# Rotation tables of a state-space scan: made per unit at their use, or all eight ahead of time and kept in DRAM

## The chip, the cores and the metric

The kernel runs on one core of a Trainium2 chip. The metric is the device time of one execution in microseconds (us), the median of several runs. The engines are named as in the profile: PE (TensorE, matmuls), DVE (VectorE), ACT (ScalarE), POOL (GpSimd) and SP (SyncE, which here issues most DMAs). Each engine, and each DMA queue, takes its instructions in the order in which they stand in its row.

## The reference

It is one layer of a hybrid decoder for 512 prompt tokens (plus 16 meta tokens) and 8 sample tokens. All of them share the weights. An attention branch and an S5 state-space branch run in parallel on parts of one projection, and are merged. What matters here is the state-space branch:

```python
lam_bar = jnp.exp(lam * dt)
b_bar = ((lam_bar - 1.0) / lam)[..., None] * lax.complex(b_re, b_im)
bu = jnp.einsum('gph,btgh->btgp', b_bar, uf)
a_cum, h = lax.associative_scan(ssm_combine, (a, bu), axis=1)
y = jnp.einsum('ghp,btgp->btgh', c, h).real + d_skip * uf
```

`lam_bar` is a complex number per group and state. The recurrence h(t) = lam_bar h(t-1) + bu(t) is linear.

## The kernel before, in words

**Stages.** The span has five stages. From 0 to 113 us the first blocks of the input projection run, each a product of a 2048 x 128 slice of weights with all tokens. From 113 to 416 us come 15 "quads" (`quad`, `Quads`): groups of four blocks of 1024 x 128 weights that are computed with seven products in place of eight, from sums of weight blocks and sums of token blocks. From 430 to 730 us come the remaining projection blocks with the state-space units between them, then attention up to 1096 us, and the output projection in quads again.

**A product** takes fp32 numbers as two parts of lower precision. For each 128 x 128 tile of weights PE does three matmuls, 24 in a product: `pr<-...,whi` twice and `pr<-...,wlo` once (L1382, in `product`). The weight parts are made just ahead (`Quads.make`, `Quads.load`): SP loads `raw` from DRAM; where a sum of weight blocks is needed DVE adds two of them (L1073, `raw<-raw`); ACT casts `raw` to `whi` (L1074); DVE subtracts, `wlo = raw - whi` (L1075), the "split". Six places for `raw` and five pairs of places for `whi` and `wlo` are used in turn. So DVE has to give one split per product, and PE's later products wait for it. DVE also adds up the results of a quad (L1417, L1422, L1432) and scales them (L1200); SP stores them to `gD`.

**Background work.** Everything else is written as Python generators (`Background`), of which `step` advances some at each product according to a credit: a `yield` names the cost of the piece before it, `yield None` ends the turn, and GBUDGET is the credit given per product. That sets the program order. A scheduler then makes each engine's row out of it, with weight work at a high priority, so that rows differ from the program order; semaphores keep what depends on each other in order. `later()` stands for `tc.issue_after(bg.last)`: what is issued inside it is to be issued after PE's latest product matmul.

**ssm_prep** runs in the background of the quads, on POOL (class `OnPool`), with small operations (mostly 128 x 32 and 128 x 64) in `work` tiles, two flat rooms `flats[0]` and `flats[1]` of 2144 numbers a partition. It computes `lam`, its powers, the factors `Fk`, and two tables of powers of the unit-modulus part of `lam_bar`: T6 (exponents 0 to 5) and T11 (multiples of 6, eleven of them). The function `powers` makes each; `norm` (L239 to L243) scales it to modulus one at the end, for T11 with operations 704 wide (L240, L243). T6[j] times T11[i] is the rotation for step 6i + j of a segment of L = 66 steps. The kept values (KEPT, 1920 numbers a partition) are stored to DRAM with one DMA of POOL's queue after the 14th quad, because x's parts need the room, and loaded again after the quads.

**ssm_consts** prepares one of eight units (four groups of states on 128 partitions each) in the state-space stage, on DVE and ACT, and at its end makes the unit's rotation table `tab` (L404 to L419): four outer products T11 x T6 (L412), a subtraction (L415) and a negated addition (L419), all 128 x 264 on DVE. **ssm_block** does the unit: PE computes bu; DVE rotates it with `tab` (p1, p2, L483 and L484; w, L488 and L489, for each half of the unit apart); scans with the real decay (L503), which leaves a scan without complex numbers; and rotates back, for each of NB = 2 segments apart (L509, L510: two products 528 wide; L512, L513: two sums 264 wide). PE then makes y.

Of the kernel before, what the change touches and what calls it, by code (L numbers as in the profile page):

```python
# [8 lines left out]
F32 = mybir.dt.float32  # L9
# [3 lines left out]
ALU = mybir.AluOpType  # L13
AX = mybir.AxisListType
P = 128
L = 66
NB = 2
NC = 132
# [49 lines left out]
def cmul(v, pool, out, a, br, bi, sh, tag):  # L68
# [13 lines left out]
KEPT = (("prm", (3, 32)), ("lam", (2, 32)), ("lamp", (2, 4, 32)), ("Fk", (8, 32)), ("nF", (2, 32)), ("r4", (32,)),  # L82
        ("T6", (2, 32, 6)), ("T11", (2, 32, 11)), ("car", (2, 32)))
NKEPT = sum(int(np.prod(s)) for _, s in KEPT)

# [51 lines left out]

def kept(ap):

    r, o = {}, 0  # L140
    for nm, sh in KEPT:
# [7 lines left out]
def ssm_prep(nc, K, tmp, psum, dram, R, ident, a_prm, later):  # L149

    v = OnPool(nc, tmp)
    prm = K["prm"]
# [4 lines left out]
    t = tmp.tile([P, 32], F32, name="th")  # L157
# [10 lines left out]
    yield 3.0  # L168
    x = tmp.tile([P, 32], F32, name="xr")
# [4 lines left out]
    v.tensor_tensor(out=th, in0=aim, in1=dt, op=ALU.mult)  # L174
    yield 3.0

# [31 lines left out]
    v.tensor_tensor(out=lam, in0=e1, in1=bc(rho, 1, 2), op=ALU.mult)  # L208
    yield 3.0

# [17 lines left out]
    v.tensor_scalar(out=nF, in0=fv[:, :, 0], scalar1=-1.0, scalar2=None, op0=ALU.mult)  # L228
    yield 2.5

# [14 lines left out]
    def powers(tab, z, cnt, tag):  # L245

        v.memset(tab[:, 0, :, 0], 1.0)
        v.memset(tab[:, 1, :, 0], 0.0)
        zs = [z]
        for i in range(3):  # L250
            nz = tmp.tile([P, 2, 32], F32, name=f"{tag}z{i}")
            cmul(v, tmp, nz, zs[-1], zs[-1][:, 0], zs[-1][:, 1], (32,), "c32_")
            zs.append(nz)
        n = 1
        for zp in zs:
            m = min(n, cnt - n)
# [5 lines left out]
            yield 1.5  # L262
        norm(tab, (32, cnt), "nt")
        yield 2.0
        return zs
# [16 lines left out]
    car = K["car"]  # L282
    v.tensor_tensor(out=car, in0=c2, in1=bc(r4, 1, 2), op=ALU.mult)
    yield 1.0
    for _ in range(8):
        yield None
# [11 lines left out]
    R["FD"] = FD  # L298
    yield 0.0


# [21 lines left out]
def ssm_consts(nc, pool, dram, R, D, ub, a_bT, a_bN, a_cT, e32, d_skip, later, free):  # L323
# [40 lines left out]
    B = pool.tile([P, 2, 512], F32, name="B")  # L364
    nc.sync.dma_start(out=B, in_=a_bT[ub])
    CL = pool.tile([P, 4, 2, 5, 32], F32, name="CL")
    nc.scalar.copy(out=CL[:, :, :, 0], in_=c)
# [35 lines left out]

    tab = pool.tile([P, 2, 4, L], F32, name="tab")  # L404
    x = R["T11"][:, :, ps]
    y = R["T6"][:, :, ps]
    t1 = pool.tile([P, 4, 11, 6], F32, name="rt1", bufs=1)
    t2 = pool.tile([P, 4, 11, 6], F32, name="rt2", bufs=1)
    tv = tab.rearrange("p r a (i j) -> p r a i j", j=6)

    def outer(dst, i, j):
        v.tensor_tensor(out=dst, in0=bc(x[:, i], 3, 6), in1=bc(y[:, j], 2, 11), op=ALU.mult)  # L412
    outer(t1, 0, 0)
    outer(t2, 1, 1)
    v.tensor_tensor(out=tv[:, 0].rearrange("p a i j -> p (a i j)"), in0=t1.rearrange("p a i j -> p (a i j)"),  # L415
                    in1=t2.rearrange("p a i j -> p (a i j)"), op=ALU.subtract)
    outer(t1, 0, 1)
    outer(t2, 1, 0)
    v.scalar_tensor_tensor(out=tv[:, 1].rearrange("p a i j -> p (a i j)"), in0=t1.rearrange("p a i j -> p (a i j)"),  # L419
                           scalar=-1.0, in1=t2.rearrange("p a i j -> p (a i j)"), op0=ALU.mult, op1=ALU.subtract)  # L420
    D["tab"] = tab
# [4 lines left out]
    D["d0"] = d0  # L426
    yield 2.4

# [15 lines left out]
def ssm_block(nc, pool, R, D, ub, y_out, later):  # L444
# [26 lines left out]
    yield 0.0  # L471
    yield None
    for h in range(2):
        p1 = pool.tile([P, 2, 2, NB, L], F32, name="p1", tag="rt1", bufs=1)
        p2 = pool.tile([P, 2, 2, NB, L], F32, name="p2", tag="rt2", bufs=1)
        for i in range(2):
            parts = [(slice(0, 2), bu[2 if h else i][:, 0:280].rearrange("p (e c) -> p e c", e=2))]
            if (h, i) == (1, 1):
                parts = [(slice(e, e + 1), place(1, 1, e).unsqueeze(1)) for e in range(2)]
            for es, b in parts:  # L480
                a = slice(2 * h + es.start, 2 * h + es.stop)
                bi = b[:, :, 0:NC].rearrange("p e (n l) -> p e n l", l=L)
                v.tensor_tensor(out=p1[:, i, es], in0=bi, in1=bc(tab[:, 0, a], 2, NB), op=ALU.mult)  # L483
                v.tensor_tensor(out=p2[:, i, es], in0=bi, in1=bc(tab[:, 1, a], 2, NB), op=ALU.mult)  # L484
                g = slice(4 * ub + a.start, 4 * ub + a.stop)
                v.tensor_tensor(out=R["sst"][:, g, i], in0=R["A0"][:, g, i], in1=b[:, :, NC:140], op=ALU.add)
        wv = w[:, :, 2 * h:2 * h + 2].rearrange("p n a r l -> p r a n l")
        v.tensor_tensor(out=wv[:, 0], in0=p1[:, 0], in1=p2[:, 1], op=ALU.subtract)  # L488
        v.tensor_tensor(out=wv[:, 1], in0=p1[:, 1], in1=p2[:, 0], op=ALU.add)  # L489
        yield 3.0  # L490
    tre, tim = bc(tab[:, 0], 2, 2), bc(tab[:, 1], 2, 2)
    for n in range(NB):
# [12 lines left out]
        yield 1.3 + 0.8 * n  # L505
    for n in range(NB):
        t1 = pool.tile([P, 4, 2, L], F32, name="rt1", bufs=1)
        t2 = pool.tile([P, 4, 2, L], F32, name="rt2", bufs=1)
        v.tensor_tensor(out=t1, in0=w[:, n], in1=tre, op=ALU.mult)  # L509
        v.tensor_tensor(out=t2, in0=w[:, n], in1=tim, op=ALU.mult)  # L510
        hs = slice(9 + n * L, 9 + n * L + L)
        v.tensor_tensor(out=H[:, :, 0, hs], in0=t1[:, :, 0], in1=t2[:, :, 1], op=ALU.add)  # L512
        v.tensor_tensor(out=H[:, :, 1, hs], in0=t2[:, :, 0], in1=t1[:, :, 1], op=ALU.subtract)  # L513
        yield 2.2
    for i, sg in ((0, 1.0), (1, -1.0)):
# [416 lines left out]
BUDGET = 6.4  # L932
GBUDGET = 0.4
BUDGET2, BUDGET3, BUDGET4 = 6.0, 3.4, 4.8
# [154 lines left out]
def trunk(tc, A, O):  # L1089
# [396 lines left out]
    def xpart(k, c):  # L1486
# [5 lines left out]
    flats = [xp.tile([P, 8 * CH], F32, name="work", tag=n) for n in ("xhq", "xlq")]  # L1492
    bg.add(ssm_prep(nc, kept(flats[0][:, 0:NKEPT]), Places([flats[1], flats[0][:, NKEPT:]], spots()), aux, dram, S, C["idn"],
                    A["prm"], lambda: tc.issue_after(bg.last)))
    kD = dram.tile([P, NKEPT], F32, name="kept")

# [453 lines left out]
```

## Time and profile before

| what | us |
|---|---|
| three runs | 1263.16, 1266.23, 1267.95 (median 1266.23) |
| span of the profiled execution (its whole time is not listed apart) | 1262.3 |
| PE busy | 1250.9 (99%) |
| DVE busy | 980.6 (78%) |
| ACT busy | 628.7 (50%) |
| POOL busy | 266.1 (21%) |
| all waits of PE for DVE in the quads | 0.2 |
| waits of PE in the state-space units | 0.6, 0.6, 0.5 |

A row of a form (a group of instructions of one line, operation and shape) reads: line, engine, operation, output <- inputs, shapes, how often; then busy time in us, mean in ns, idle time ahead of them on the engine, and what ended it. A row of the timeline reads: start, duration, what; in brackets the idle time before it and what released it. A row of a window reads: from, to, length, then busy time of PE, PE's weight loads, DVE, ACT and POOL with the number of instructions of each, PE's granted clock, the busy share of the DMA engines, and GB/s.

### The profile page before, as it was taken

How to read it: one execution, taken by the hardware profiler on the slowest of the kernel's cores; microseconds unless marked ns; L12 is line 12 of the kernel's file. 1: busy time of each engine (PE TensorE's matmuls, PEld its weight loads, DVE VectorE, ACT ScalarE, POOL GpSimd, SP SyncE). 2: the span in 40 equal slices, each digit the busy share in tenths (PEclk: the TensorE clock that was granted, in tenths of full speed). 3: DMA queues.
4: the chain of work that ended last, by engine and by line, in shares of the span. 5: the costliest groups of instructions: out<-in, count | busy, mean ns of one | idle time of the engine just before them, and what ended most of it. 6: DMA issues, size and time to landing. Idle time of an engine off the chain costs nothing.

```text
span 1262.3 us, 26537 instructions
## 1 busy us (share of the span) xinstructions
PE 1250.9 (99%) x10357; PEld 1227.7 (97%) x10357; DVE 980.6 (78%) x1554; ACT 628.7 (50%) x1344; POOL 266.1 (21%) x437
## 2 busy tenths in 40 slices
PE   9999999999999999999999999999999999999998
PEld 9999999999999999999999999999999999999998
DVE  8687878887778668888897377899887577887875
ACT  8554445444545586556432235567555333344342
POOL 0003999940000033122220123211011000000000
PEclk9999999999999999999999989999999999999999
DMA  8544343443434656555554775777666756555441
GB/s 294 199 160 153 134 143 110 143 150 134 151 126 146 214 172 182 159 165 167 156 159 121 246 211 182 224 240 225 189 214 203 258 174 189 165 192 163 145 139 51
DMA packets 108001, 219.22 MB, mean 174 GB/s; under 512 B 21932, under 2 KB 47492, under 8 KB 107844
## 3 DMA queue, kind: packets, MB, share of 16 engines
q1 hardware_dynamic: 99172, 198.53, 48.5%
q0 software_dynamic: 8704, 19.00, 5.6%
q8 instruction: 81, 1.33, 0.4%
q14 instruction: 44, 0.36, 0.1%
HBM read 181.57 MB, written 36.82 MB: 173 GB/s over the span
## 4 chain that ended last, share of the span: by engine, by line
PE 92%; DVE 3%; DMA 2%; ACT 1%; SPq 1%; issue 0%; DVEq 0%; ACTq 0%
PE mm L1168 45%; PE pr L1382 35%; PE wg L854 2%; PE mm L1255 2%; PE aux L1382 1%; PE aux L1168 1%; PE aux L1255 1%; DVE wlo L1009 1%; PE aux L806 1%; PE aux L805 1%; ACT ct L346 1%; PE tr L526 1%; PE tr L836 1%; PE wg L526 1%; DMA Y<-yD 0%
## 5 line engine op out<-in xcount | busy, mean ns | idle before, releaser
L1075 DVE TENSOR_TENSOR wlo<-raw,whi 128x1024 fp32r<-128x1024 f32 x161 | 198.5, 1253 | 69.6 <-ACT whi L1074 69.0
L1074 ACT CAST whi<-raw 128x1024 fp32r<-128x1024 f32 x161 | 166.4, 1049 | 167.2 <-DVE raw L1073 80.0
L1168 PE MATMUL mm<-xh,whi 128*128 128x260 f32 (+1 forms) x792 | 185.8, 288 | 3.1 <-DVE t L563 2.9
L1008 ACT CAST whi<-raw 128x1024 fp32r<-128x1024 f32 (+3 forms) x128 | 122.3, 965 | 132.3 <-PE mm L1168 85.6
L1168 PE MATMUL mm<-xh,wlo 128*128 128x260 f32 (+1 forms) x792 | 184.4, 287 | 0.0
L1168 PE MATMUL mm<-xl,whi 128*128 128x260 f32 (+1 forms) x792 | 184.1, 286 | 0.0
L1009 DVE TENSOR_TENSOR wlo<-raw,whi 128x1024 fp32r<-128x1024 f32 (+3 forms) x128 | 142.2, 1119 | 46.5 <-ACT whi L1008 45.7
L1382 PE MATMUL pr<-tau,whi 128*128 128x260 f32 x928 | 168.6, 283 | 0.0
L1382 PE MATMUL pr<-cb,whi 128*128 128x260 f32 x848 | 153.0, 283 | 0.0
L1382 PEld LDWEIGHTS pr<-tau,whi 128*128 128x128 f32 x928 | 143.0, 188 | 0.0
L1168 PEld LDWEIGHTS mm<-xh,whi 128*128 128x128 f32 x792 | 132.5, 189 | 5.8 <-ACT KH L747 3.1
L1168 PEld LDWEIGHTS mm<-xl,whi 128*128 128x128 f32 x792 | 133.1, 190 | 0.4 <-issue 0.4
L1168 PEld LDWEIGHTS mm<-xh,wlo 128*128 128x128 f32 x792 | 132.2, 189 | 0.4 <-issue 0.4
L1382 PEld LDWEIGHTS pr<-cb,whi 128*128 128x128 f32 x848 | 130.8, 188 | 0.2 <-ACT z L1416 0.2
L1382 PE MATMUL pr<-tau,wlo 128*128 128x260 f32 x464 | 130.8, 282 | 0.0
L1382 PE MATMUL pr<-cb,wlo 128*128 128x260 f32 x424 | 119.1, 283 | 0.2 <-DVE wlo L1075 0.2
L1073 DVE TENSOR_TENSOR raw<-raw 128x1024 f32<-128x1024 f32 x91 | 113.9, 1252 | 1.6
L1168 PE MATMUL mm<-Y,whi 128*128 128x260 f32 x576 | 105.1, 287 | 0.0
L1382 PE MATMUL pr<-xl,whi 128*128 128x260 f32 x352 | 98.9, 283 | 0.0
L1382 PE MATMUL pr<-xh,wlo 128*128 128x260 f32 x352 | 98.8, 283 | 0.0
L1382 PE MATMUL pr<-xh,whi 128*128 128x260 f32 x352 | 97.1, 283 | 0.0
L1382 PEld LDWEIGHTS pr<-tau,wlo 128*128 128x128 f32 x464 | 87.2, 188 | 0.0
(421 smaller groups left out, 2974.9 us busy)
## 6 DMA issues: line engine op xcount, KB each, us to landing
raw<-in_w SPq DMA_DIRECT2D x202, 512.0 KB, 4.3
gD<-z SPq DMA_DIRECT2D x34, 260.0 KB, 4.3
t<-gD SPq DMA_DIRECT2D x32, 260.0 KB, 3.1
cache<-in_vc POOLq DMA_DIRECT2D x16, 286.0 KB, 3.5
cache<-in_kc POOLq DMA_DIRECT2D x15, 288.0 KB, 4.0
xr<-in_x SPq DMA_DIRECT2D x16, 268.0 KB, 6.5
xg<-in_x SPq DMA_DIRECT2D x8, 536.0 KB, 4.7
sbw<-rawD SPq DMA_DIRECT2D x16, 260.0 KB, 5.1
```

The costliest lines, as they stand in the source:

```text
L346: nc.scalar.activation(out=dst, in_=src, func=AF.Copy, scale=x)
L526: nc.tensor.matmul(o[n], lhsT=D["CL"][:, 2 * e + n, i, 1:5], rhs=H[:, 2 * e + n, i, 0:140], start=False, stop=(i == 1))
L805: nc.tensor.matmul(ps[:, e, 0:272], lhsT=q, rhs=KH[:, k0:k0 + 272], start=True, stop=False)
L854: nc.tensor.matmul(pv[64 * e:64 * e + 64, 0:256], lhsT=V, rhs=pr[:, e::2], start=(i == 0), stop=(i == len(parts) - 1))
L1008: nc.scalar.copy(out=hi, in_=raw)
L1009: self.dve = nc.vector.tensor_tensor(out=lo, in0=raw, in1=hi.bitcast(F32), op=ALU.subtract).ins
L1073: nc.vector.tensor_tensor(out=o, in0=o, in1=i, op=ALU.add)
L1074: nc.scalar.copy(out=hi, in_=t)
L1075: nc.vector.tensor_tensor(out=lo, in0=t, in1=hi.bitcast(F32), op=ALU.subtract)
L1168: m = nc.tensor.matmul(ps[:, c, 0:W], lhsT=wt[:, k], rhs=xo(kt, c), start=f, stop=l)
L1255: nc.tensor.matmul(ps[:, c, 0:260], lhsT=wt[:, kt % 8], rhs=xk(xo, kt, c, 8), start=f, stop=l)
L1382: m = nc.tensor.matmul(bank, lhsT=wt[:, p], rhs=x(p, e), start=first and f and p == 0, stop=l and p == 7, skip_group_check=not first and l ...
```

## The change

T6 and T11 leave the kept values, so that the DMA that stores and loads them is 832 numbers a partition in place of 1920. At the end of `ssm_prep` all eight rotation tables are made, on DVE, in `room`, which is `flats[1]`: into `t[0]` the products with one of T6's two parts, into `t[1]` those with the other, combined in place in `t[0]`. Each table is stored twice side by side (r = 0, 1) into `tabD` in DRAM by two DMAs of SP's queue, in pieces of 66 numbers (264 bytes), 1024 pieces and 264 KB each. The yields of `ssm_prep` are about halved, the pause ahead of `ft` goes from 8 to 14 turns, and GBUDGET from 0.4 to 0.5. `ssm_consts` no longer makes the table, but loads it with one DMA. `ssm_block` takes both halves in one subtraction and one addition (528 wide), and both segments in one operation each of the rotation back (1056 and 528 wide).

```diff
-        ("T6", (2, 32, 6)), ("T11", (2, 32, 11)), ("car", (2, 32)))
+        ("car", (2, 32)))
+MADE = KEPT + (("T6", (2, 32, 6)), ("T11", (2, 32, 11)))
...
-    for _ in range(8):
+    for _ in range(14):
         yield None
...
+    R["tabD"] = dram.tile([8, P, 16 * L], F32, name="tabD")
+    t = [f.rearrange("p (r a i j) -> p r a i j", r=2, a=4, j=6) for f in (room[:, 0:8 * L], room[:, 8 * L:16 * L])]
+    for ub in range(8):
+        ps = slice(4 * ub, 4 * ub + 4)
+        with later():
+            for r in range(2):
+                for e in range(2):
+                    v_.tensor_tensor(out=t[r][:, e], in0=bc(T11[:, e, ps], 3, 6), in1=bc(T6[:, r, ps], 2, 11), op=ALU.mult)
+            a, b = (f.rearrange("p r a i j -> p r (a i j)") for f in t)
+            v_.tensor_tensor(out=a[:, 0], in0=a[:, 0], in1=b[:, 1], op=ALU.subtract)
+            v_.scalar_tensor_tensor(out=a[:, 1], in0=a[:, 1], scalar=-1.0, in1=b[:, 0], op0=ALU.mult, op1=ALU.subtract)
+            d = R["tabD"][ub].rearrange("p (x r l) -> p x r l", r=2, l=L)
+            for r in range(2):
+                nc.sync.dma_start(out=d[:, :, r], in_=t[0].rearrange("p r a i j -> p (r a) (i j)"))
+        yield 2.4
...
+    tab = pool.tile([P, 2, 4, 2, L], F32, name="tab")
+    nc.sync.dma_start(out=tab.rearrange("p i a r l -> p (i a r l)"), in_=R["tabD"][ub])
...
-    outer(t1, 0, 0)
-    outer(t2, 1, 1)
...
-    yield 2.4
+    yield 0.0
...
-        wv = w[:, :, 2 * h:2 * h + 2].rearrange("p n a r l -> p r a n l")
-        v.tensor_tensor(out=wv[:, 0], in0=p1[:, 0], in1=p2[:, 1], op=ALU.subtract)
-        v.tensor_tensor(out=wv[:, 1], in0=p1[:, 1], in1=p2[:, 0], op=ALU.add)
+    wv = w.rearrange("p n a r l -> p r a n l")
+    v.tensor_tensor(out=wv[:, 0], in0=p1[:, 0], in1=p2[:, 1], op=ALU.subtract)
+    v.tensor_tensor(out=wv[:, 1], in0=p1[:, 1], in1=p2[:, 0], op=ALU.add)
...
-    for n in range(NB):
-        t1 = pool.tile([P, 4, 2, L], F32, name="rt1", bufs=1)
...
+    t1 = pool.tile([P, NB, 4, 2, L], F32, name="rt1", bufs=1)
+    t2 = pool.tile([P, NB, 4, 2, L], F32, name="rt2", bufs=1)
+    for t, i in ((t1, 0), (t2, 1)):
+        v.tensor_tensor(out=t.rearrange("p n a r l -> p n (a r l)"), in0=w.rearrange("p n a r l -> p n (a r l)"),
+                        in1=bc(tab[:, i].rearrange("p a r l -> p (a r l)"), 1, NB), op=ALU.mult)
...
-GBUDGET = 0.4
+GBUDGET = 0.5
```

Lines after the new code are 4 to 19 higher than before (the split L1075 is L1079 after, the sum L1073 is L1077, the scaling L1200 is L1204, POOL's L243 is L244).

**The first place** is DVE's row at the passage from the third quad's results to the fourth quad's (`z` and `t` are the results of quads in turn, `pr_...` the PSUM banks they come from). Before:

```order
L1200 TENSOR_TENSOR z<-z,R 128x520
L1075 TENSOR_TENSOR wlo<-raw,whi 128x1024 x5
L1073 TENSOR_TENSOR raw<-raw 128x1024 x2
L1417 TENSOR_TENSOR t<-t,pr_2273 128x260
L1075 TENSOR_TENSOR wlo<-raw,whi 128x1024
L1422 TENSOR_TENSOR t<-t,pr_2276 128x260
L1073 TENSOR_TENSOR raw<-raw 128x1024
L1200 TENSOR_TENSOR t<-t,R 128x520
```

After, in the same place (`work<-work` are the table operations):

```order
L1204 TENSOR_TENSOR z<-z,R 128x520
L1079 TENSOR_TENSOR wlo<-raw,whi 128x1024 x3
L308 TENSOR_TENSOR work<-work 128x264 x4
L1079 TENSOR_TENSOR wlo<-raw,whi 128x1024
L311 SCALAR_TENSOR_TENSOR work<-work 128x264
L310 TENSOR_TENSOR work<-work 128x264
L1079 TENSOR_TENSOR wlo<-raw,whi 128x1024
L308 TENSOR_TENSOR work<-work 128x264 x2
L1077 TENSOR_TENSOR raw<-raw 128x1024
L1421 TENSOR_TENSOR t<-t,pr_2361 128x260
L1077 TENSOR_TENSOR raw<-raw 128x1024
L1426 TENSOR_TENSOR t<-t,pr_2364 128x260
```

The first four table operations stand behind three splits, and all later splits stand behind them; the 48 operations of the eight tables are spread over the rows of this quad and the three that follow it. The first of them waits for POOL's L244 of T11, the operation 704 wide.

**The second place** is SP's queue at the same time, after (before, only `raw` loads and stores to `gD` stand there). The DMAs to `tabD` are the stores of the tables:

```order
L1056 DMA raw<-in_w 128x1024 x2
L314 DMA tabD<-work 1024x1x66 x2
L1211 DMA gD<-t 128x520
L1056 DMA raw<-in_w 128x1024
L314 DMA tabD<-work 1024x1x66 x2
L1211 DMA gD<-t 128x520
```

The stores stand between the loads of weights, two per table.

**The third place** is DVE's row in the state-space stage, where the first unit is prepared. Before:

```order
L375 TENSOR_TENSOR B<-rt_5513,rt_5514 128x512
L412 TENSOR_TENSOR rt_5577<-kept 128x264
L412 TENSOR_TENSOR rt_5578<-kept 128x264
L415 TENSOR_TENSOR tab<-rt_5577,rt_5578 128x264
L412 TENSOR_TENSOR rt_5577<-kept 128x264
L412 TENSOR_TENSOR rt_5578<-kept 128x264
L419 SCALAR_TENSOR_TENSOR tab<-rt_5577,rt_5578 128x264
L1009 TENSOR_TENSOR wlo<-raw,whi 128x1024
```

After:

```order
L393 TENSOR_TENSOR B<-rt_5580,rt_5581 128x512
L394 TENSOR_TENSOR B<-rt_5580,rt_5581 128x512
L1013 TENSOR_TENSOR wlo<-raw,whi 128x1024
L1210 SCALAR_TENSOR_TENSOR z<-t,z 128x520
L1013 TENSOR_TENSOR wlo<-raw,whi 128x1024
```

The six operations that made `tab` are gone.

More of the change, by code (lines that the diff above doesn't have):

```diff
@@ L82 @@
 KEPT = (("prm", (3, 32)), ("lam", (2, 32)), ("lamp", (2, 4, 32)), ("Fk", (8, 32)), ("nF", (2, 32)), ("r4", (32,)),
-        ("T6", (2, 32, 6)), ("T11", (2, 32, 11)), ("car", (2, 32)))
-NKEPT = sum(int(np.prod(s)) for _, s in KEPT)
+        ("car", (2, 32)))
+MADE = KEPT + (("T6", (2, 32, 6)), ("T11", (2, 32, 11)))
+NKEPT, NMADE = (sum(int(np.prod(s)) for _, s in t) for t in (KEPT, MADE))
 def shaped(ap, sh):
@@ L135, in spots, with kept @@
     return r
-def kept(ap):
+def kept(ap, names=KEPT):
     r, o = {}, 0
-    for nm, sh in KEPT:
+    for nm, sh in names:
         n = int(np.prod(sh))
@@ L146, in kept, with ssm_prep @@
     return r
-def ssm_prep(nc, K, tmp, psum, dram, R, ident, a_prm, later):
+def ssm_prep(nc, K, tmp, psum, dram, R, ident, a_prm, later, room):
     v = OnPool(nc, tmp)
@@ L167, in ssm_prep @@
     acc_exp(v, tmp, dt, ldt, 32)
-    yield 3.0
+    yield 1.6
     x = tmp.tile([P, 32], F32, name="xr")
@@ L174, in ssm_prep @@
     v.tensor_tensor(out=th, in0=aim, in1=dt, op=ALU.mult)
-    yield 3.0
+    yield 1.6
     magic = 12582912.0
@@ L228, in ssm_prep @@
     v.tensor_scalar(out=nF, in0=fv[:, :, 0], scalar1=-1.0, scalar2=None, op0=ALU.mult)
-    yield 2.5
+    yield 1.3
     r4 = K["r4"]
@@ L261, in powers @@
             n += m
-            yield 1.5
+            yield 0.8
         norm(tab, (32, cnt), "nt")
-        yield 2.0
+        yield 1.0
         return zs
@@ L365, in ssm_consts @@
     nc.sync.dma_start(out=B, in_=a_bT[ub])
+    tab = pool.tile([P, 2, 4, 2, L], F32, name="tab")
+    nc.sync.dma_start(out=tab.rearrange("p i a r l -> p (i a r l)"), in_=R["tabD"][ub])
+    D["tab"] = tab
     CL = pool.tile([P, 4, 2, 5, 32], F32, name="CL")
@@ L505, in ssm_block @@
         yield 1.3 + 0.8 * n
-    for n in range(NB):
-        t1 = pool.tile([P, 4, 2, L], F32, name="rt1", bufs=1)
[L508 to L514, printed above, removed]
+    t1 = pool.tile([P, NB, 4, 2, L], F32, name="rt1", bufs=1)
[3 more added lines that the diff above has]
+                        in1=bc(tab[:, i].rearrange("p a r l -> p (a r l)"), 1, NB), op=ALU.mult)
+    yield 2.5
+    hv, v1, v2 = (t.rearrange(f"p {o} -> p r a n l", l=L) for t, o in
+                  ((H[:, :, :, 9:9 + NC], "a r (n l)"), (t1, "n a r l"), (t2, "n a r l")))
+    v.tensor_tensor(out=hv[:, 0], in0=v1[:, 0], in1=v2[:, 1], op=ALU.add)
+    v.tensor_tensor(out=hv[:, 1], in0=v2[:, 0], in1=v1[:, 1], op=ALU.subtract)
+    yield 1.4
     for i, sg in ((0, 1.0), (1, -1.0)):
@@ L1492, in trunk @@
     flats = [xp.tile([P, 8 * CH], F32, name="work", tag=n) for n in ("xhq", "xlq")]
-    bg.add(ssm_prep(nc, kept(flats[0][:, 0:NKEPT]), Places([flats[1], flats[0][:, NKEPT:]], spots()), aux, dram, S, C["idn"],
-                    A["prm"], lambda: tc.issue_after(bg.last)))
+    bg.add(ssm_prep(nc, kept(flats[0][:, 0:NMADE], MADE), Places([flats[1], flats[0][:, NMADE:]], spots()), aux, dram, S,
+                    C["idn"], A["prm"], lambda: tc.issue_after(bg.last), flats[1]))
     kD = dram.tile([P, NKEPT], F32, name="kept")
```

30 lines of the change are left out of this document (8 added, 22 removed).

## The prediction

> **What bounds the kernel now.** I read the page first. TensorE (PE) is busy for the whole span; VectorE (DVE) has a fifth of its time free. GpSimd (POOL) is idle for most of the span, but its row of tenths (40 slices of 31.6 us) shows a block of full slices.
>
> ```profile
> span 1262.3 us, 26537 instructions
> PE 1250.9 (99%) x10357; PEld 1227.7 (97%) x10357; DVE 980.6 (78%) x1554; ACT 628.7 (50%) x1344; POOL 266.1 (21%) x437
> POOL 0003999940000033122220123211011000000000
> ```
>
> The chain of waits says when the seven-product groups run. Their first product starts at 113.47, and from 139.10 on the chain stays on PE for 191.59 us.
>
> ```profile
> 113.47 2.87 PE aux L1382 x24
> 139.10 191.59 PE pr L1382 x1594
> ```
>
> 191.59 / 1594 is 0.1202 us a matmul, so a product of 24 takes 2.885 us and a group of seven 20.2 us. Product n (from 0) is due at 113.47 + 2.885 n. The waits of PE show how little there is to win: one of 0.2 us in all groups, and in the state-space stage three of 0.6, 0.6 and 0.5. The longest, 2.9, comes after that stage, at the per-head norms.
>
> ```profile
> PE mm L1168 <- DVE t L563: 2.9, 1, 2.9
> PE tr L526 <- DVE H L512: 0.6, 1, 0.6
> PE aux L1349 <- DVE sst L486: 0.6, 1, 0.6
> PE tr L523 <- DVE sst L486: 0.5, 1, 0.5
> PE pr L1382 <- DVE wlo L1075: 0.2, 1, 0.2
> ```
>
> The windows (PE, PEld, DVE, ACT, POOL busy, then granted clock, DMA share, GB/s) give the stages: all groups, a stretch inside them that matters below, and the stretch around the 2.9 us wait.
>
> ```profile
> 113.00:413.00 300.00, 300.00 (x2498) 300.00 (x2498) 244.11 (x244) 145.48 (x204) 146.81 (x205) 1.00 0.40 136
> 183.10:261.90 78.80, 78.80 (x658) 78.80 (x657) 67.00 (x63) 35.89 (x50) 78.33 (x105) 1.00 0.38 131
> 700.00:770.00 70.00, 67.06 (x541) 66.31 (x540) 43.70 (x95) 23.56 (x42) 18.08 (x31) 0.95 0.77 231
> ```
>
> **What goes away in the state-space stage.** By form, in 430 to 700 us:
>
> ```profile
> L412 DVE TENSOR_TENSOR rt<-kept 128x264 f32<-128x264 f32 x32 | 12.3, 425 | 0.1
> L419 DVE SCALAR_TENSOR_TENSOR tab<-rt,rt 128x264 f32<-128x264 f32 x8 | 3.4, 431 | 0.2
> L488 DVE TENSOR_TENSOR w<-p,p 128x264 f32<-128x264 f32 x16 | 6.8, 424 | 0.0
> L509 DVE TENSOR_TENSOR rt<-w,tab 128x528 f32<-128x528 f32 x16 | 11.2, 700 | 0.1
> L372 DVE TENSOR_TENSOR rt<-B,f 128x1024 f32<-128x1024 f32 x8 | 9.8, 1225 | 2.1 <-issue 1.9
> ```
>
> Each of eight units loses its table build: four products of 0.425 and two combinations of 0.43, 2.56 us. The rotations do the same elements in fewer operations: eight 264 wide become four 528 wide (8 x 0.425 - 4 x 0.70 = 0.6), and four 528 wide become two 1056 wide (4 x 0.70 - 2 x 1.25 = 0.3, by the 1024-wide row): 0.9 us a unit. DVE is freed of 8 x 3.46, about 28 us. PE saw only 0.6 + 0.6 + 0.5 = 1.7 us of waits there, so the gain on the path is **-1.7 us**, and at least 0. The new load of each table lands well ahead; the smaller copy of the kept values hides behind the last group. The 2.9 us wait follows other work, and I leave it.
>
> **What the build costs where it goes.** The 48 table operations stand in DVE's row from the fourth group on (the first place shown above). The first needs the 11-step power table from POOL, whose last operation is the 704-wide one of L243 before (L244 after). DVE runs its row in order. Behind the waiting operation stand all later weight splits (wlo), and behind those every later product of PE; the sums (raw) that ACT casts stand there too. The request to issue after PE's last product orders nothing on DVE. When does DVE arrive, and when is POOL done? The timelines of DVE and POOL:
>
> ```profile
> 178.17 0.72 DVE L1200 TENSOR_TENSOR z<-z,R 128x520 f32<-128x520 f32 x1
> 179.42 3.70 DVE L1075 TENSOR_TENSOR wlo<-raw,whi 128x1024 fp32r<-128x1024 f32 x3 [0.53 <-ACT whi L1074]
> ...
> 186.60 1.23 DVE L1075 TENSOR_TENSOR wlo<-raw,whi 128x1024 fp32r<-128x1024 f32 x1 [1.59 <-ACT whi L1074]
> ```
>
> ```profile
> 185.19 0.32 POOL L75 TENSOR_TENSOR work<-work 128x64 f32<-128x64 f32 x1
> ...
> 186.46 0.38 POOL L228 TENSOR_SCALAR work<-work 128x64 f32<-128x64 f32 x1
> 186.80 1.21 POOL L75 TENSOR_TENSOR work<-work 128x64 f32<-128x64 f32 x1
> 246.49 0.57 POOL L76 TENSOR_TENSOR work<-work 128x192 f32<-128x192 f32 x1
> 247.03 0.25 POOL L77 TENSOR_TENSOR work<-work 128x32 f32<-128x32 f32 x1
> 259.67 2.17 POOL L243 TENSOR_TENSOR work<-work 128x704 f32<-128x704 f32 x1
> ```
>
> DVE is there at 179.42 + 3.70 = 183.1, after the splits of products 0 to 27 (28 of them stand before the first table operation). POOL finished that table at 261.84. If POOL kept its pace, DVE would stand for 79 us. It will not: the window 183.10:261.90 holds 105 POOL operations, back to back (78.33 of 78.80), beside 67.00 us of DVE; the form rows there are
>
> ```profile
> L75 POOL TENSOR_TENSOR work<-work 128x64 f32<-128x64 f32 x17 | 13.9, 822 | 0.2
> L77 POOL TENSOR_TENSOR work<-work 128x32 f32<-128x32 f32 x17 | 12.8, 750 | 0.3
> L76 POOL TENSOR_TENSOR work<-work 128x64 f32<-128x64 f32 x17 | 12.2, 723 | 0.0
> L78 POOL TENSOR_TENSOR work<-work 128x32 f32<-128x32 f32 x17 | 8.6, 507 | 0.0
> ```
>
> The same 64-wide operation takes 0.32 or 1.21. The fast run of six from 185.19 to 186.80 lies where DVE was idle (its next split, at 186.60, waited for ACT), 1.61 / 6 = 0.27 us each. With DVE standing, all run so. The 68 operations of the four rows, 47.5 us now, take 68 x 0.27 = 18.4. The other 37 took 78.3 - 47.5 = 30.8; I halve them, since they are wider (192 wide starts every 0.54): 15.4. For pairs that wait for each other I add 2.4. Sum 36.2 (bounds 32 and 42): POOL is done at 183.1 + 36.2 = **219.3**.
>
> The Trainium skill, SBUF — State Buffer, section "SBUF: two separate sides", says that a VectorE operation with two SBUF inputs and a GpSimd one that reads SBUF take a shared port pair as an exclusive lock for the whole instruction. That agrees with 0.32 against 1.21; by it, POOL's speed-up would be full.
>
> PE meanwhile runs until product 28 is due, at 113.47 + 28 x 2.885 = 194.2, and stops. Then DVE has to do its row in order, with the table operations in it. Durations by form, 113 to 413 us:
>
> ```profile
> L1075 DVE TENSOR_TENSOR wlo<-raw,whi 128x1024 fp32r<-128x1024 f32 x103 | 128.6, 1270 | 42.7 <-ACT whi L1074 42.3
> L1073 DVE TENSOR_TENSOR raw<-raw 128x1024 f32<-128x1024 f32 x58 | 73.6, 1269 | 1.0
> L1200 DVE TENSOR_TENSOR t<-t,R 128x520 f32<-128x520 f32 x14 | 10.8, 772 | 0.0
> L1432 DVE TENSOR_TENSOR t<-t,pr 128x520 f32<-128x520 f32 x7 | 4.9, 694 | 3.7 <-PE pr L1382 3.7
> L1417 DVE TENSOR_TENSOR t<-t,pr 128x260 f32<-128x260 f32 x7 | 2.9, 417 | 0.0
> ```
>
> The first split after the stand comes 4 x 0.43 + 1.25 = 3.0 later, at 222.3: PE is **28 us** late. DVE does not win this back, for in this stretch it has more work than PE. From the first table operation to the split of product 47 the row holds 44 table operations (18.9 us), 20 splits at 1.25 (25.0), 12 sums at 1.27 (15.2), 6 scalings at 0.75 (4.5), and 9 additions of results (3 x 0.694 + 6 x 0.417 = 4.6): 68.2 us. The split of product 47 is done at 219.3 + 68.2 = 287.5; PE wanted it at 113.47 + 47 x 2.885 = 249.1. That is **38.4 us** late, the most anywhere in the row (at product 31 it is 33). Afterwards a group costs DVE 7 x 1.25 + 4 x 1.27 + 3.0 = 16.8 of PE's 20.2, so no more is lost, and nothing is given back, because PE has no spare time later.
>
> Two costs I put at nothing. After the 2.9 us pause of PE, which lies in it, the window 700:770 has clock 0.95, so 5% of 70 us, 3.5 us, are lost to a slower clock; after a 28 us stop the same can come again. But here PE waits for DVE's splits for another 60 us, and a slower product or two hides in those waits (without them: +3.5). The Trainium skill, TensorE: Matmul & The Clock Gate, Part 1, puts the clock at half after about 3.4 us of idling until about 3.4 us of work, which would make 1.7 us each time; the trace shows more for a shorter pause.
>
> The other is the tables' stores. Each build sends two of 264 KB through SP's queue, in 264-byte pieces, and stands there ahead of the next weight loads; the next build may overwrite the first room only when they have been read. In DVE's row some 7.5 us lie between (a split 1.25, two products 0.86, two sums 2.54, two additions 0.83, a split 1.25, a scaling 0.77). The nearest store:
>
> ```profile
> gD<-z SPq DMA_DIRECT2D x34, 260.0 KB, 4.3
> ```
>
> Two of them at 4.3, overlapping, land inside 7.5 us; in a row they need 8.6, which would be 1.1 us more at each of seven builds, +8. I take 0 and keep 8 for the range.
>
> **The sum.** +38.4 - 1.7 = **+36.7 us**. The profiled span is 1262.3, which would become 1299.0. Its own whole time is not listed; the three runs shown, 1263.16 to 1267.95, lie 0.9 to 5.7 above the span, the median 1266.23 lies 3.9 above. Forecast: 1266.2 + 36.7 = **1303**. Its own range, by POOL's 32 to 42, DVE's waits for ACT (42.3 us on 103 splits, 0.41 each; if they stayed on the 20 splits, +8) and a lighter DVE beside an idle POOL (-3): 1294 to 1315.
>
> **Rivals.**
> - *Catching up costs more* (0.17). The stores land late: +8 by the row above, and SP's queue keeps the weight loads behind them; or the slower clock returns at each pause. The trace has no store in such short pieces to weigh it by; the DMA share of 0.38 in this stretch speaks against it. 1308 to 1330, middle 1318. The Trainium skill, DMA: Bandwidth & Descriptors, Specifications, asks for at least 512 B a transfer and says that shorter ones are read, modified and written; if that doubled a landing of 8.6 to 17, it would be +9.7 at each of seven builds, 1371, beyond my range. No store of this trace shows it; inside this rival I give that end 0.03.
> - *POOL does not speed up* (0.05). Then DVE stands until 261.8; 42.5 later than above, and 1345. Against it speak the 0.27 us operations.
> - *A smaller loss* (0.06): POOL's wide operations are as quick as the narrow ones (105 x 0.27 = 28) and DVE gains 3 beside an idle POOL, so 1303 - 11 = 1292; if half of the table operations (10 us) also fall into waits for ACT that DVE would have had anyway, 1282.
> - *Faster, the other side* (0.03). The wait costs nothing if POOL has the table when PE would run dry, at 194.2 less the 3.0 for table operations and split: 105 operations in 8 us, under 0.08 us each. Or if DVE has not arrived by then. The rest would be -1.7, and with the 2.9 us pause and its 3.5 us of clock gone too, -8: 1258 to 1264. The deciding point is POOL's pace, 0.08 against 0.27 seen.
> - *The change does not do what it says* (0.03): something holds the table operations until the last groups, where POOL is long done (261.84 of 416). DVE has 42.7 us of waits in the groups, the 48 x 0.43 = 20.6 us of builds fit in, and the time stays at 1264 to 1268. The order of DVE's row speaks against it.
>
> **How the numbers follow.** The forecast has 0.66. The range reaches down to 1286, so that it holds half of the smaller loss, and up to 1320, with some 0.10 of the dearer catching up; outside are about 0.2. About 0.5%, 6.3 us, is what a measurement of this kernel can tell from no change. Slower by more than that are the forecast, the dearer one, the slow POOL and the smaller loss: 0.94. Within it: 0.03, the change that does nothing. Faster: 0.03.
>
> **What would show it.** In the profile of the changed kernel: a wait of DVE at L308 for POOL's L244 of some 36 us from 183 on, POOL's operations at 0.27 in it and done at about 219; PE waiting for wlo, first for 28 us from 194 and then for about 10 in smaller pieces up to 290; the groups ending at about 455 instead of 113.47 + 15 x 20.2 = 416.5; the state-space stage without its waits of 0.5 and 0.6. Wrong would be: no wait at L308 or one under 15 us; POOL still at 0.8 while DVE stands; DVE waiting for the stores of the table; or a loss of PE after 300 us.

## The result, and the profile after

The changed kernel takes 1310.49 us (median of four runs, 1308.97 to 1315.64), the kernel before 1265.83 beside it: a ratio of 1.0361, with a 95% interval of 1.0337 to 1.0386. It is 45 us slower. The profiled execution has a span of 1307.2 us, and its own time is 1308.97. The forecast was 1303, in a range of 1286 to 1320.

The page of the profile after shows the hole in the tenths of PE (the seventh slice, from 196 to 229 us), and GpSimd done two slices earlier than before:

```profile
span 1307.2 us, 26511 instructions
PE 1258.0 (96%) x10357; PEld 1231.9 (94%) x10357; DVE 969.1 (74%) x1506; ACT 628.5 (48%) x1344; POOL 219.9 (17%) x437
...
PE   9999982989999999999999999999999999999998
...
POOL 0004997000000013222222023212011100000000
PEclk9999995999999999999999999999999999999999
```

PE's waits, the longest groups. The first row replaces one of 0.2 us; its longest single wait is 29.8:

```profile
PE pr L1386 <- DVE wlo L1079: 34.3, 6, 29.8
PE mm L1172 <- DVE t L567: 2.8, 1, 2.8
PE aux L410 <- DVE sst L488: 2.1, 1, 2.1
PE pr L1386 <- ACT whi L1078: 1.5, 3, 0.7
```

VectorE's own waits name what stands behind that: once for GpSimd's table, and seven times for the stores:

```profile
DVE work L308 <- POOL work L244: 35.3, 1, 35.3
DVE work L308 <- DMA tabD<-work: 13.4, 7, 3.3
```

VectorE's timeline at the stand, in the order in which the row was shown ahead of the prediction:

```profile
179.17 3.76 DVE L1079 TENSOR_TENSOR wlo<-raw,whi 128x1024 fp32r<-128x1024 f32 x3 [0.44 <-ACT whi L1078]
218.23 1.71 DVE L308 TENSOR_TENSOR work<-work 128x264 f32<-128x264 f32 x4 [35.31 <-POOL work L244]
219.87 1.21 DVE L1079 TENSOR_TENSOR wlo<-raw,whi 128x1024 fp32r<-128x1024 f32 x1
221.00 0.42 DVE L311 SCALAR_TENSOR_TENSOR work<-work 128x264 f32<-128x264 f32 x1
221.34 0.42 DVE L310 TENSOR_TENSOR work<-work 128x264 f32<-128x264 f32 x1
```

GpSimd in the stand, by form from 183 to 218.3 us, and the operation that ends it. The same 68 small operations that took 47.5 us beside VectorE take 19.2 alone:

```profile
L76 POOL TENSOR_TENSOR work<-work 128x64 f32<-128x64 f32 x17 | 5.3, 317 | 0.0
L75 POOL TENSOR_TENSOR work<-work 128x64 f32<-128x64 f32 x17 | 5.3, 316 | 0.2
L77 POOL TENSOR_TENSOR work<-work 128x32 f32<-128x32 f32 x17 | 4.3, 254 | 0.3
L78 POOL TENSOR_TENSOR work<-work 128x32 f32<-128x32 f32 x17 | 4.3, 254 | 0.0
```

```profile
216.53 1.67 POOL L244 TENSOR_TENSOR work<-work 128x704 f32<-128x704 f32 x1
```

The windows of the stop, of the first work after it, and of the catching up (columns as before; the eighth number is the granted clock):

```profile
191.40:221.20 29.80, 0.07 (x1) 0.07 (x1) 2.97 (x6) 0.00 (x0) 28.47 (x82) 0.57 0.01 4
221.20:229.00 7.80, 6.79 (x30) 6.49 (x31) 7.18 (x12) 1.68 (x2) 0.00 (x0) 0.50 0.60 111
229.00:300.00 71.00, 65.15 (x512) 63.26 (x512) 58.16 (x86) 28.43 (x40) 0.00 (x0) 0.97 0.79 166
270.00:280.00 10.00, 6.70 (x45) 6.24 (x44) 6.71 (x13) 3.73 (x7) 0.00 (x0) 0.86 0.66 109
```

PE stands for 29.8 us, then works 7.8 us at half clock, and then still misses 5.9 us of the next 71. The last row lies inside those 71: after another wait, of 2.6 us, the clock falls once more. From 113 to 470 us PE's waits come to 36.5 us. PE is 43.8 late at the end of the groups, so 7.3 us are not waiting; most of them are the slower clock.

PE's matmuls are the same 10357 in the same order in every kernel here, so each can be placed: how much later does the 3300th (near the end of the groups) and the 7500th (after the state-space stage and the per-head norms) start than in the kernel before, at 401.4 and 912.5? One profile of each kernel:

```
kernel               3300th   7500th   median us   ratio to before (95%)
changed               +43.8    +44.9     1310.49   1.0361 (1.0337 to 1.0386)
wait_only             +30.9    +31.7     1294.90   1.0240 (1.0217 to 1.0264)
long_rows             +35.6    +36.2     1301.67   1.0295 (1.0271 to 1.0320)
behind_split_late      +4.9     +4.1     1267.53   1.0023 (1.0007 to 1.0038)
late_long_rows         -0.1     +3.2     1267.17   1.0017 (1.0009 to 1.0026)
late_pool_loads        +0.2     +2.0     1266.27   1.0016 (1.0005 to 1.0027)
late_old_rotation      -0.4     +6.2     1270.01   1.0044 (1.0030 to 1.0059)
behind_split_48       +17.9    +25.0     1288.60   1.0183 (1.0170 to 1.0196)
pool_builds           +68.0    +72.3     1339.81   1.0593 (1.0563 to 1.0624)
pool_queue             +2.1     +5.2     1269.99   1.0052 (1.0034 to 1.0070)
old_rotation           +9.2    +15.0     1275.54   1.0079 (1.0057 to 1.0100)
no_tables              +0.1     +0.2     1264.03   0.9992 (0.9982 to 1.0002)
```

In the changed kernel 43.8 of the 44.9 us are there before the state-space stage begins. After that it gains nothing back.

### The profile page after: what moved, and what is told of

It reads as the page before. It is cut to its first block, busy times and chain, and to the rows that moved or that the text cites. A ratio compares the mean times of both kernels' runs of the same rounds, so it can differ in the third digit from the quotient of the medians.

```text
span 1307.2 us, 26511 instructions
## 1 busy us (share of the span) xinstructions
PE 1258.0 (96%) x10357; PEld 1231.9 (94%) x10357; DVE 969.1 (74%) x1506; ACT 628.5 (48%) x1344; POOL 219.9 (17%) x437
## 4 chain that ended last, share of the span: by engine, by line
PE 49%; DMA 1%; DVE 1%; SPq 0%; issue 0%; ACT 0%; DVEq 0%
PE mm L1172 30%; PE pr L1386 12%; PE wg L858 2%; PE aux L810 1%; PE aux L809 1%; PE mm L1697 1%; PE tr L840 1%; PE aux L1386 0%; DMA rb<-rkD 0%; PE mm L1688 0%; PE wg L530 0%; PE tr L530 0%; DMA rawD<-z 0%; DMA z<-sqD 0%; PE aux L410 0%
## 5 line engine op out<-in xcount | busy, mean ns | idle before, releaser
L1079 DVE TENSOR_TENSOR wlo<-raw,whi 128x1024 fp32r<-128x1024 f32 x161 | 194.3, 1226 | 58.2 <-ACT whi L1078 57.5
L1386 PE MATMUL pr<-tau,whi 128*128 128x260 f32 x928 | 171.5, 286 | 1.7 <-DVE t L1421 1.0
L1077 DVE TENSOR_TENSOR raw<-raw 128x1024 f32<-128x1024 f32 x91 | 111.3, 1223 | 1.3
L1386 PEld LDWEIGHTS pr<-xh,wlo 128*128 128x128 f32 x352 | 66.3, 190 | 31.4 <-DVE wlo L1079 31.3
```

The lines of the kernel that those rows point to most:

```text
L1077: nc.vector.tensor_tensor(out=o, in0=o, in1=i, op=ALU.add)
L1079: nc.vector.tensor_tensor(out=lo, in0=t, in1=hi.bitcast(F32), op=ALU.subtract)
L1386: m = nc.tensor.matmul(bank, lhsT=wt[:, p], rhs=x(p, e), start=first and f and p == 0, stop=l and p == 7, skip_group_check=not first and l ...
```

## Experiments

The theory was that VectorE, taking its row in order, stands at the first table operation for GpSimd's T11, and that all later splits, and so PE, stand behind it. The rivals were the table work itself, the stores, and the merged rotation.

**The wait alone.** The kernel before, with one operation added after T11 is made:

```diff
     Zs = yield from powers(T11, Z, 11, "zb")
+    v_.tensor_copy(out=T11[:, 0, 0, 0:1], in_=T11[:, 0, 0, 0:1])
```

> The kernel before plus one copy of a single column on VectorE that reads T11 after its scaling (128x1, in place): the wait alone, without table work, stores or any change in the state-space stage. It stands in VectorE's row behind the same 28 splits. My theory (the stand behind GpSimd is the loss): a stand of 34 to 36 us from 183 on, GpSimd done at about 218, a first stop of PE of 28 to 30, some 3 to 4 more for the slow clock afterwards, nothing given back: 1294 to 1300. Rival (the table work, the stores or the merged rotation carry the loss): no change, 1264 to 1270.

Measured: 1294.90. VectorE's timeline, and the windows of PE's stop and of its restart:

```profile
218.01 0.15 DVE L276 COPY work<-work 128x1 f32<-128x1 f32 x1 [35.37 <-POOL work L243]
218.12 2.48 DVE L1076 TENSOR_TENSOR wlo<-raw,whi 128x1024 fp32r<-128x1024 f32 x2
```

```profile
191.40:219.20 27.80, 0.00 (x0) 0.00 (x0) 1.19 (x2) 0.00 (x0) 27.64 (x79) 0.55 0.00 0
219.20:226.00 6.80, 6.53 (x31) 6.24 (x32) 6.73 (x9) 1.05 (x1) 2.31 (x3) 0.56 0.35 146
```

One copy of 0.15 us on one column costs 31 us, two thirds of the whole change. The stop is 28 of them; the half clock after it makes up the rest (6.8 us at 0.56 are 3.0). VectorE then has time to spare again, and still nothing is won back, since PE has none.

**The same table work, but later.** `later(1)` names VectorE's latest split in place of PE's latest product, and the tables are emitted 14 products later:

```diff
-    for _ in range(14):
+    for _ in range(28):
...
-        with later():
+        with later(1):
...
-                    C["idn"], A["prm"], lambda: tc.issue_after(bg.last), flats[1]))
+                    C["idn"], A["prm"], lambda n=0: tc.issue_after(qs.dve if n else bg.last), flats[1]))
```

> The changed kernel with the table operations issued after VectorE's own latest split instead of PE's latest product, and emitted 14 products later; they then stand behind 62 splits. My theory: GpSimd has the table at 262 or before, VectorE comes there at about 280, so no wait for GpSimd; the 20.6 us of table work and some waits for the stores take VectorE's spare time, PE loses 0 to 6 in the groups, and the state-space stage costs 1 as in the changed kernel: 1266 to 1274. Rival (the table work in the groups and its stores are the loss, wherever they stand): 1285 or more.

Measured: 1267.53. GpSimd ends T11 as in the kernel before, and the table operations follow a split without any wait for it:

```profile
259.94 2.17 POOL L244 TENSOR_TENSOR work<-work 128x704 f32<-128x704 f32 x1
```

```profile
280.59 2.36 DVE L1079 TENSOR_TENSOR wlo<-raw,whi 128x1024 fp32r<-128x1024 f32 x2 [0.56 <-ACT whi L1078]
282.87 1.46 DVE L308 TENSOR_TENSOR work<-work 128x264 f32<-128x264 f32 x4
```

The 48 operations are the same, the stores are the same, and 41 of the 45 us are gone (44.9 less 4.1). What is left in the groups, 4.9, goes with waits for the stores:

```profile
DVE work L308 <- DMA tabD<-work: 10.7, 5, 3.8
```

**Stores in long rows.** The changed kernel with the table stored once as it lies, 2112 bytes a partition, and doubled by two loads:

```diff
-            d = R["tabD"][ub].rearrange("p (x r l) -> p x r l", r=2, l=L)
-            for r in range(2):
-                nc.sync.dma_start(out=d[:, :, r], in_=t[0].rearrange("p r a i j -> p (r a) (i j)"))
+            nc.sync.dma_start(out=R["tabD"][ub], in_=t[0].rearrange("p r a i j -> p (r a i j)"))
...
-    nc.sync.dma_start(out=tab.rearrange("p i a r l -> p (i a r l)"), in_=R["tabD"][ub])
+    for r in range(2):
+        nc.sync.dma_start(out=tab[:, :, :, r].rearrange("p i a l -> p (i a) l"), in_=R["tabD"][ub].rearrange("p (x l) -> p x l", l=L))
```

> The changed kernel with each table stored once, in rows of 2112 bytes, and doubled by two loads in the state-space stage. Table operations stand where they stood. If the stores in 264-byte pieces hold VectorE up while it catches up (13.4 us of waits at L308 for tabD): these waits fall under 4 us and the time to 1302 to 1306. If the waits for the stores are filled from elsewhere (ACT's casts): within 2 of the changed kernel, 1308 to 1312.

Measured: 1301.67. The DMA issues from 215 to 300 us of the changed kernel (queue, count, KB each, median us to landing), and then of this one, with VectorE's wait:

```profile
tabD<-work SPq DMA_DIRECT2D x16, 264.0 KB, 7.0
```

```profile
tabD<-work SPq DMA_DIRECT2D x8, 264.0 KB, 3.0
```

```profile
DVE work L308 <- DMA tabD<-work: 1.4, 2, 1.2
```

The short stores cost 13.4 - 1.4 = 12.0 us of VectorE's waits, and 43.8 - 35.6 = 8.2 us of PE: 5.2 of waits (36.5 against 31.3 from 113 to 470 us) and 3.0 that is not waiting. The two times to landing are medians of few landings, three and two, since the trace has no others. This run changes both the length of a piece and the number of stores, and the packets in the traces show that both count. The bytes are halved; and a packet of 264 bytes took 29 ns on average from 215 to 300 us, one of 2112 bytes 88 ns, so the short ones took 2.6 times as long for the same bytes.

What remains above `wait_only`, 35.6 - 30.9 = 4.7, comes with the table work in VectorE's row: 1.5 of a longer stop (29.8 against 28.3), 1.5 of later waits, and 1.7 that is not waiting.

**Later and long rows together.** Both edits above.

> As behind_split_late, with the stores in rows of 2112 bytes and two loads per unit. VectorE's waits for the stores fall from 10.7 to under 3, PE's loss in the groups from 4.8 to 0 to 3: 1262 to 1267. If the stores do not matter there: 1266 to 1270, as behind_split_late.

Measured: 1267.17. In the groups nothing is lost any more (-0.1 at the 3300th matmul), and VectorE's waits for the stores are down to 0.5. The time did not fall below `behind_split_late`, because this profile is 3.3 us later in the state-space stage.

**The first table behind 48 splits.** The same edit as `behind_split_late`, with the 14 left as in the changed kernel:

> As behind_split_late, but emitted where the changed kernel emits them: the first table operation stands behind 48 splits, where VectorE comes at about 240 and GpSimd would be done at 262 beside it. By my theory the stand is about 10, since GpSimd speeds up again; VectorE is four products (11.5) ahead, so PE does not stop at once; but then the row holds 92.8 us of work and some 11 of waits for stores for 89 us of PE: 10 + 92.8 + 11 - 89.4 - 11.5 = 13 lost in the groups, 1272 to 1282. If a stand costs PE its whole length, 1283 or more; if only a stop of PE counts, 1264 to 1269.

Measured: 1288.60, above what I expected. The stand itself came as worked out, shorter than the 21 us that GpSimd would have needed beside VectorE:

```profile
240.22 2.73 DVE L1079 TENSOR_TENSOR wlo<-raw,whi 128x1024 fp32r<-128x1024 f32 x2
251.87 1.72 DVE L308 TENSOR_TENSOR work<-work 128x264 f32<-128x264 f32 x4 [8.91 <-POOL work L244]
```

```profile
253.00:331.00 78.00, 67.55 (x508) 66.08 (x507) 64.55 (x93) 27.89 (x38) 0.80 (x1) 0.91 0.74 157
```

PE is 17.9 late at the end of the groups, where 13 were expected. Its waits in the groups come to 11.3, near the 13. The other 6.6 are not waiting; the window of the catching up has a granted clock of 0.91, and 9% of its 78 us is 7.0. That sum had no slower clock in it. Another 7 come in the state-space stage, which I had left out. So a stand of 8.9 that uses up VectorE's lead costs more than its own length, when the work that it delays fills the row behind it and PE's stops bring the slower clock.

**Tables on GpSimd, stores still on SP's queue.**

```diff
-                    v_.tensor_tensor(out=t[r][:, e], in0=bc(T11[:, e, ps], 3, 6), in1=bc(T6[:, r, ps], 2, 11), op=ALU.mult)
+                    v.tensor_tensor(out=t[r][:, e], in0=bc(T11[:, e, ps], 3, 6), in1=bc(T6[:, r, ps], 2, 11), op=ALU.mult)
```

(the subtractions likewise, the negation as an operation of its own).

> The changed kernel with the table operations on GpSimd (seven a table, the negation apart) and the stores still in SP's queue. VectorE has no wait for GpSimd. My theory (an engine that takes its row in order stands, whichever it is): now SP stands behind the first table with the weight loads behind it, PE runs dry some 25 us later than in the changed kernel, and the loss is still 25 to 40: 1290 to 1306. Rival (only VectorE's row matters): 1264 to 1270.

Measured: 1339.81, worse than I expected, by the mechanism that I expected. SP's queue waits, VectorE's longest wait, and GpSimd's price for one product:

```profile
SPq L315 <- POOL work L312: 128.8, 8, 53.0
```

```profile
245.22 2.85 DVE L1078 TENSOR_TENSOR raw<-raw 128x1024 f32<-128x1024 f32 x2 [37.36 <-DMA raw<-in_w]
```

```profile
L308 POOL TENSOR_TENSOR work<-work 128x264 f32<-128x264 f32 x32 | 32.7, 1037 | 44.1 <-DMA tabD<-work 43.6
```

SP stands behind the first table for 53.0 us, with the weight loads behind it; VectorE gets its next weights at 245. I had counted that one stand. But there are eight: each later table costs GpSimd four products of 1.04 us, three more operations and a wait for the store of the one before (43.6 in all), keeps SP again (128.8 - 53.0 = 75.8 us more), and the loss grows from 37 at the 1800th matmul to 68. In the changed kernel SP's queue stood behind the first table too, for 38.5 us; no wait of VectorE or ACT for weights shows there.

**Tables on GpSimd, stores in long rows on its own queue.** Neither VectorE's row nor SP's queue stands for GpSimd's tables then.

> Table operations on GpSimd and the stores, one per table in rows of 2112 bytes, on GpSimd's own queue; two loads per unit in the state-space stage. No row of VectorE or SP stands for GpSimd. My theory: PE loses at most 1 in the groups, and what is left is the state-space stage, -1 to +2: 1262 to 1267. Rival (making the tables beside the groups costs by itself, through the shared port or the DMA): 1272 or more.

Measured: 1269.99, above the 1262 to 1267 of my theory, below the 1272 of the rival. PE is 2.1 late at the end of the groups and 5.2 after the state-space stage. The 2.1 come at one place, and a row does stand for GpSimd there, which I had overlooked. By the profile it is ACT's: its copy at L296 waits for GpSimd's L78, the copy out of a PSUM bank (L1398) stands behind it, and PE waits for that one.

```profile
247.46 0.37 ACT L296 COPY work<-tr 128x256 f32<-128x256 f32 x1 [4.15 <-POOL work L78]
248.68 0.39 ACT L1398 ACTIVATE z<-pr 128x260 f32<-128x260 f32 x1
```

```profile
249.12 0.39 PE L1386 MATMUL pr<-xh,whi 128*128 128x260 f32 x1 [1.72 <-ACT z L1398]
```

VectorE's operations get longer as well: from 215 to 320 us, beside GpSimd, a split takes 1455 ns, where it takes 1219 from 222 to 300 us of the changed kernel, with GpSimd idle. PE has no wait for a split in the groups of this kernel, so there this costs it nothing.

```profile
L1079 DVE TENSOR_TENSOR wlo<-raw,whi 128x1024 fp32r<-128x1024 f32 x36 | 51.2, 1455 | 8.5 <-ACT whi L1078 7.9
```

```profile
L1079 DVE TENSOR_TENSOR wlo<-raw,whi 128x1024 fp32r<-128x1024 f32 x23 | 27.9, 1219 | 0.0
```

**The rotation as before.** `pool_queue`, and then `late_long_rows`, with each half of a unit and each segment rotated apart, as in the kernel before.

> As pool_queue, but the rotations as in the kernel before: each half of the unit and each segment apart. My theory: the merged rotation frees 7 us of VectorE that PE does not wait for, so this is within 2 of pool_queue. Rival (the longer operations make PE wait for sst and for the groups of matmuls behind it, 2.1 at the bias matmuls in the changed kernel): 2 to 4 faster than pool_queue.

> As late_long_rows (1267, PE 3 late after the state-space stage), but the rotations as in the kernel before, each half and each segment apart. If the merged rotation is what makes PE late in that stage: 1263 to 1265 and no loss there. If it is the loads of the tables or only the arrangement: within 2 of late_long_rows.

Measured: 1275.54 and 1270.01, against 1269.99 and 1267.17 with the merged rotation. Both are slower, by 5.6 and 2.8, which neither expectation had. Of the first pair's difference most lies in the groups, 9.2 late against 2.1 in these profiles, although no operation is edited there. It begins with the same stand of ACT at L296, 5.9 us in this profile against 4.2. PE's stop behind it is 3.0 in place of 1.7, and this time the clock falls after it:

```profile
250.00:252.00 2.00, 1.86 (x8) 1.86 (x9) 2.00 (x2) 1.02 (x2) 2.00 (x4) 0.52 0.91 224
```

PE is 4.6 late after that; another 4.6 come from 270 to 280 us, with waits for a cast and for a split (0.9 and 1.7) and a clock of 0.79 from 272 to 280. The second pair has no loss in the groups. Within the state-space stage the old rotation is later than the merged one in both pairs, by 2.7 and 3.3 us, so the merged rotation is not what makes PE late there.

**No tables at all.** The kernel before, with GpSimd setting `tab` to ones in place of the six operations of each unit; the rotation is by ones then, so that the state-space results are not computed.

```diff
-    outer(t1, 0, 0)
-    outer(t2, 1, 1)
...
+    nc.gpsimd.memset(tab, 1.0)
```

> The kernel before without the six table operations of each unit: the rotation table is set to ones by GpSimd, so nothing is built, stored or loaded. It is the most that freeing VectorE of the builds can give in the state-space stage. My theory (three waits of PE, 1.7 us, are all there is): PE's waits in that stage fall to between 0 and 1.7, 1262 to 1266, the same as before within 2. Rival (the builds hold PE up in ways its waits do not show): under 1260. If the arrangement of the stage alone moves PE by some us either way: up to 1269.

Measured: 1264.03, a ratio of 0.9992 (0.9982 to 1.0002): no difference. PE's waits between 425 and 800 us in this kernel, in which VectorE has 20 us less to do:

```profile
PE mm L1153 <- DVE t L548: 3.3, 1, 3.3
PE tr L511 <- DVE H L497: 2.5, 2, 2.2
PE aux L391 <- ACT z L1337: 1.0, 1, 1.0
```

They are not shorter than before, they lie elsewhere.

**The loads of the tables on GpSimd's queue.** `late_long_rows`, with `nc.gpsimd` in place of `nc.sync` for the two loads of `tab`.

> As late_long_rows (1267, PE 3 late after the state-space stage), but the two loads of each unit's table go through GpSimd's queue instead of SP's. If it is the place of these loads in SP's queue, ahead of weights and constants, that makes PE late there: no loss in that stage, 1263 to 1265. If it is the arrangement of the stage's rows, which a changed queue alters too: anywhere within 3 of late_long_rows, and PE's waits fall at other places.

Measured: 1266.27, within 1 of `late_long_rows`, and 2.0 late at the 7500th matmul in place of 3.2. The place of the loads in SP's queue is not shown to be the cause.

## Why the prediction was right, point by point

- **When VectorE comes, and when GpSimd is done**: 183.1 and 219.3 forecast. Measured: the last split before the stand ends at 179.17 + 3.76 = 182.9, and the table operation starts at 218.23. The speed-up of GpSimd, from 47.5 to 18.4 us for the 68 small operations, was 19.2.
- **The stop of PE**: 28 forecast, from 194.2 on; 29.8 measured, from 191.4. The stop begins one product sooner, and VectorE's row has the reason: splits are not made in the order of the products. Ahead of the stand VectorE had made 28 splits, but PE had run the `wlo` matmuls of 27 products when it stopped, so one of the 28 belongs to a later product.
- **The slower clock at nothing**: wrong. The forecast let it hide in PE's waits for splits. It did not hide: 7.3 of PE's 43.8 us are not waiting, 4.3 of 35.6 with long rows, 2.6 of 30.9 in `wait_only`, and most of that is the clock (the row 221.20:229.00 has 0.50 for 7.8 us). The Trainium skill, TensorE: Matmul & The Clock Gate, Part 1, gives about 3.4 us of work until full clock; the trace has 7.8, so the row decides.
- **Catching up**: far too dear. 10.4 were forecast beyond the stop (38.4 less 28.0), all of them waits; with long rows the waits beyond the stop are 1.5. The operations were counted rightly, but they fill the row less than I worked out. In the changed kernel the stretch from the first table operation to the split of product 47 lasts 72.4 us, from 218.2 to 290.6, and 12.4 of them are waits, nearly all for the stores. So the work takes 60.0 where I had 68.2. The durations add up to 66.8, but neighbouring operations overlap in the profile by some 0.07 us each (at 221.00 one of 0.42 starts, at 221.34 the next), and I had added whole durations. Splits and sums took 1.22 each with GpSimd idle, against the 1.25 and 1.27 that I used.
- **The stores at nothing**: the step that failed. The forecast kept 8 us for them as a bound, in a rival with 0.17, and named a wait of VectorE for the stores as a sign of being wrong. That sign came: they cost VectorE 13.4 us of waits, and PE 8.2. A store of 264 KB in 264-byte pieces, one of two at once, took 7.0 to land, where I used 4.3 from a store in pieces of 2080 bytes.
- **The state-space stage, -1.7**: not seen. The changed kernel goes from +43.8 to +44.9, a small loss after 300 us, which the prediction had named as a sign of being wrong. `no_tables` shows that taking the builds out of this stage gives nothing: the waits that were there move to other places. Kernels that load tables are 0.8 earlier to 7.1 later at its end than at its start. `wait_only`, whose stage is not edited, has a wait of 3.0 in it that the kernel before does not have. What makes PE late there by some us is not settled: the merged rotation and the queue of the loads were tried and are not shown to be it.

So the mechanism, its place and its first term were right: 29.8 of the 44.9 us are the stop. That the sum came within 8 us is partly luck. The stop was 1.8 longer, the stores cost 8.2, the clock 4.3 even without them, and the stage is 2.8 off (+1.1 against -1.7). That is 17.1 too little. Against it stands one term that was 8.9 too dear, the waits of the catching up. Without that error the forecast would have been lower still, near 1294. The 1310 also lies in the range of the rival "catching up costs more" (1308 to 1330), whose +8 for the stores is what happened; the forecast and that rival were not two separate cases.

No version here that computes the result is faster than the kernel before. The nearest, `late_pool_loads`, is at 1.0016 (1.0005 to 1.0027).

## What to carry to other kernels

Work that is moved "into the time of" another stage goes into the rows of its engines, and a row is in order: ask first when its inputs are ready on the chip, not whether the engine has time to spare. A single 0.15 us operation with a late input, ahead of the work that feeds a saturated engine, cost 31 us here, and moved behind it the whole table work cost 0 to 5 in the groups. Look at every row for such a wait, those of ACT and of the DMA queues too: two kernels that had freed VectorE's row lost by one in SP's queue and one in ACT's row. An order that names an instruction of another engine, as `later()` did with PE's product, does not hold an operation back in its own row; naming VectorE's own split did (28 splits ahead became 48 in `behind_split_48`).

## What the runs showed of the hardware

- GpSimd and VectorE slow each other, both ways. GpSimd's 64-wide product takes 0.32 us with VectorE idle and 0.72 to 0.82 on average beside it. VectorE's split takes 1219 ns with GpSimd idle, 1383 beside its small operations (183 to 262 us of the kernel before), and 1495 beside its 264-wide ones (265 to 355 us of `pool_queue`).
- The clock fell after short stops of PE too: to 0.52 after one of 3.0 us (`old_rotation`), to 0.86 on average over the 10 us around one of 2.6 (the changed kernel), but not after the one of 1.7 in `pool_queue`.
- A store in 264-byte pieces, one of two at once, took 7.0 us to land, one of the same 264 KB in rows of 2112 bytes 3.0; a packet moved 9 bytes per ns in the first case and 24 in the second. The Trainium skill, DMA: Bandwidth & Descriptors, Specifications, sets 512 bytes as the least for full rate; that agrees, and was only a rival in the prediction.
